# A decoder trunk on one core: two first sums over the memory interleaved by halves of their channels, and the fetches of constants and activations begun later

## The chip, the cores and the metric

The kernel runs on one core of one Trainium2 chip. The metric is the device time of one execution in microseconds (us). TensorE (PE in the profile) does the matrix products, VectorE (DVE), ScalarE (ACT) and GpSimd (POOL) the elementwise work, SyncE (SP) issues most of the transfers.

## The reference

Two layers over 1024 positions of 1024 channels. Each layer is a mixer (dilated attention with pooling in layer 0, a spatial gating unit with a state-space model in layer 1) and a cross-attention of four heads into 256 memory tokens. What the change touches is the memory side of that cross-attention and the first norm of x:

```
mem_n = rms_norm(mem, mem_norm)
kv = (mem_n @ w_kv).reshape(b, m, 2, X_HEADS, X_HEAD_DIM)
k, v = kv[:, :, 0], kv[:, :, 1]
sc = einsum('bshd,bmhd->bhsm', h @ w_q, k) * (X_HEAD_DIM ** -0.5)
p = softmax(sc); o = einsum('bhsm,bmhd->bshd', p, v); return o @ w_o
hn = rms_norm(x, norm_ab[0])     # layer 0's mixer starts from it
```

## The kernel before, in words

**Arithmetic.** Every matrix operand is split into a high and a low part, and a product is three matmuls: high by high, high by low, low by high (`mm3`, L206, L207, L208). For a weight, `split` makes the high part `wh` on ScalarE (L171, L180) and the low part `wl` on VectorE (L172, L181). For the memory, `norm_in` makes the pair `mg` (L226 on ScalarE, L227 on VectorE) for each of the eight channel blocks k.

**The prologue** does not need x. For both layers, `fold` multiplies the memory by `w_kv` (part 0: eight sums for the keys), folds `w_q` into the result, multiplies by the other half of `w_kv` (part 1: eight sums for the values), and folds `w_o` in. A sum over the memory is 24 matmuls of 256 columns: eight channel blocks of three. Results of the folding (`mo`, `vo`) are stored to HBM by ScalarE's queue. The sums rotate over three tags of PSUM with two banks each (`pm`, tags mm, s, o), so six sums can stand before the first bank has to be free again. A bank is freed when `kt` (L421, VectorE) has read it, and `kt` multiplies by `Rm`, the reciprocal norm of the memory. ScalarE and GpSimd then split `kt` into `ktr` (L213 and L214), the operand of the folding with `w_q`.

**Rm** comes from a chain: eight squares of the memory (`norm_sq`: L236 and L239 on ScalarE), seven additions on GpSimd (L243), and `norm_end` (L245 to L262): a high and low part (`acch`, `accl`), two matmuls with ones, logarithm and exponential on ScalarE, one multiplication on GpSimd, two steps on VectorE, the last at L262. The squares carry an ordering edge that puts them behind one chosen instruction of ScalarE, the high part of the first weight's second half.

**Weights** come in the order of a plan. `pump` loads up to `deep[0]` weights ahead of the last split and splits up to `deep[1]` ahead of the one in use; both are 5 in the prologue. Only the first weight is loaded in two halves of its channels (L158, 256 KB each) so that its first half can start early. The memory is fetched in four transfers of two channel blocks on ScalarE's queue (L366).

**Order.** The program is traced into a scheduler, which fixes the order on each engine from a simulated timeline and from the order of tracing; each engine then runs its list in order. `drive` interleaves the prologue with a side program, `pro_side`: one step of the side for every four yields of the main (rate 0.25). The prologue has 128 yields, thus 32 steps. `pro_side` lets one step pass, fetches the constants `cst` (L460), and then `load_x` fetches sixteen blocks of x (L474), one a step, splits them into `xg` (L226, L227), adds their squares, and makes the two norms with `norm_sum_pe` and `norm_sum_end` (two halves h of the positions). The reciprocal root of these norms is a chain of twelve operations on GpSimd (`rsqrt_aside`, L300 to L303), after which VectorE picks columns (L327, L329) and refines them (L289 to L293) into `Rt`. Layer 0's mixer (`ab_main`) uses `xg` in its first matmuls and `Rt` in copying their results out (L523): tiles 0 to 3 use the first half, tiles 4 to 7 the second.

Tiles of the pool tagged u (14 buffers) hold x, the squares, `kt`, `mo` and `vo` alike; a fetch of x waits until a buffer is free.

Of the kernel before, what the change touches and what calls it, by code (L numbers as in the profile page):

```python
# [8 lines left out]
F32 = mybir.dt.float32  # L9
F32R = mybir.dt.float32r  # L10
AF = mybir.ActivationFunctionType
ALU = mybir.AluOpType
# [5 lines left out]
NB = 42  # L18
# [80 lines left out]
class Prog:  # L99
# [49 lines left out]
            else:  # L149
                break  # L150

    def load(s, half=None):
        _, ap, w = s.plan[s.n_load]
        if half is not None:

            if half == 0:
                s.st[0] = s.pool.tile([128, 1024], F32, name="wst", tag="b", bufs=NB)
            s.nc.sync.dma_start(s.st[0][:, 512 * half:512 * half + 512], ap[:, 512 * half:512 * half + 512])  # L158
            s.n_load += half
            return  # L160
        t = s.pool.tile([128, 1024], F32, name="wst", tag="b", bufs=NB)
        s.last_load = s.nc.sync.dma_start(t[:, :w], ap() if callable(ap) else ap)
        s.st[s.n_load] = t
        s.n_load += 1

    def split(s, i, half=None):
        if half is not None:
            if half == 0:
                s.W[0] = [s.pool.tile([128, 1024], F32R, name=x, tag="b", bufs=NB) for x in ("wh", "wl")]
            c = slice(512 * half, 512 * half + 512)  # L170
            s.last_hi = s.nc.scalar.activation(s.W[0][0][:, c], s.st[0][:, c], AF.Copy)  # L171
            s.nc.vector.tensor_tensor(s.W[0][1][:, c], s.st[0][:, c], s.W[0][0][:, c], op=ALU.subtract)  # L172
            if half:
                s.st.pop(0)
                s.n_split += 1
            return
        t, w = s.st.pop(i), s.plan[i][2]
        H = s.pool.tile([128, 1024], F32R, name="wh", tag="b", bufs=NB)
        L = s.pool.tile([128, 1024], F32R, name="wl", tag="b", bufs=NB)
        s.last_hi = s.nc.scalar.activation(H[:, :w], t[:, :w], AF.Copy)  # L180
        s.nc.vector.tensor_tensor(L[:, :w], t[:, :w], H[:, :w], op=ALU.subtract)  # L181
        s.W[i] = (H, L)
        s.n_split += 1
# [175 lines left out]
    def constants(s):  # L359
        nc = s.nc  # L360
        s.gains = s.keep("gains", 72)
        nc.sync.dma_start(s.gains, s.a["gains"])
        s.memx = [s.b("mem0"), s.b("mem1")]
        for j in range(4):
            c = slice(512 * (j % 2), 512 * (j % 2) + 512)
            nc.scalar.dma_start(s.memx[j // 2][:, c], s.a["memT"][:, 512 * j:512 * j + 512])  # L366
            if j < 2:
                s.load(j)
        s.load()
        s.onef = s.keep("onef", 128)  # L370
        nc.vector.memset(s.onef, 1.0)
        s.ones = s.keep("ones", 128, F32R)
        nc.scalar.activation(s.ones, s.onef, AF.Copy)
        for h in range(2):
            s.R[h] = s.keep(f"R{h}", 512)
        s.Rt = s.keep("Rt", 8)
        s.mag8 = s.keep("mag8", 16)
        s.cst = s.keep("cst", C_END)
        s.ident = s.cst[:, C_ID:C_ID + 128]

    def memory(s):
        nc = s.nc
        st = {"g": G_MEM}
        mg = []
        xs = [s.memx[k // 4][:, 256 * (k % 4):256 * (k % 4) + 256] for k in range(8)]
        for k in range(8):
            if k in (2, 4):
                s.split(0, k // 2 - 1)
                first = s.last_hi
            if k % 2 == 0:  # L390
                t = s.b(f"mg{k}", F32R).rearrange("p (a b m) -> p a b m", a=2, b=2)
            mg.append((t[:, k % 2, 0], t[:, k % 2, 1]))
            s.norm_in(st, k, xs[k], 256, mg[-1], sq=False)
        s.pump()
        with s.tc.issue_after(first.ins):
            for k in range(8):
                s.norm_sq(st, k, xs[k], 256)
        s.memx = None
        s.mg = mg
        Rm = s.u("Rm")  # L400
        s.Rm = Rm[:, :256]
        s.mst = st

    def fold(s, l):

        nc = s.nc
        msc = s.dt(f"msc{l}", [2, 4, 128, 1024])
        vsc = s.dt(f"vsc{l}", [8, 128, 1024])
        s.msc[l], s.vsc[l] = msc, vsc
        for part in range(2):  # L410
            kt = []
            for d in range(8):
                key = ("kv", l, 8 * part + d)
                H, L = s.get(key)
                p = s.pm()
                yield from s.mm3(p[:, :256], [((H[:, 128 * k:128 * k + 128], L[:, 128 * k:128 * k + 128]), s.mg[k]) for k in range(8)])
                s.free(key)
                if l == 0 and part == 0 and d == 0:
                    s.norm_end(s.mst, s.Rm, 256)
                t = s.u("kt")  # L420
                nc.vector.scalar_tensor_tensor(t[:, :256], p[:, :256], 1.0 / 16 if part == 0 else 1.0, s.Rm, op0=ALU.mult, op1=ALU.mult)  # L421
                if d % 2 == 0:
                    o = s.b("ktr", F32R).rearrange("p (a b m) -> p a b m", a=2, b=2)
                kt.append((o[:, d % 2, 0], o[:, d % 2, 1]))
                s.hilo(kt[-1][0], kt[-1][1], t[:, :256], nc.gpsimd)
                yield 1
            if part == 0:
                for ct in range(8):
                    key = ("q", l, ct)
                    H, L = s.get(key)  # L430
                    for hp in range(2):
                        p = s.pm()
                        for h2 in range(2):
                            ds_ = [4 * hp + 2 * h2, 4 * hp + 2 * h2 + 1]
                            yield from s.mm3(p[:, 256 * h2:256 * h2 + 256], [((H[:, 128 * d:128 * d + 128], L[:, 128 * d:128 * d + 128]), kt[d]) for d in ds_])
                        t = s.u("mo")
                        nc.scalar.activation(t, p, AF.Copy)
                        nc.scalar.dma_start(msc[hp, ct // 2][:, 512 * (ct % 2):512 * (ct % 2) + 512], t)
                        yield 1
                    s.free(key)  # L440
            else:
                for h in range(4):
                    for oh in range(2):
                        key = ("o", l, 2 * h + oh)
                        H, L = s.get(key)
                        for mt in range(2):
                            p = s.pm()
                            yield from s.mm3(p, [((kt[2 * h + e][0][:, 128 * mt:128 * mt + 128], kt[2 * h + e][1][:, 128 * mt:128 * mt + 128]),
                                                  (H[:, 512 * e:512 * e + 512], L[:, 512 * e:512 * e + 512])) for e in range(2)])
                            t = s.u("vo")  # L450
                            nc.scalar.activation(t, p, AF.Copy)
                            kk = 2 * h + mt
                            nc.scalar.dma_start(vsc[4 * oh:4 * oh + 4, :, 128 * kk:128 * kk + 128].rearrange("c p o -> p c o"), t.rearrange("p (c o) -> p c o", c=4))
                            yield 1
                        s.free(key)

    def pro_side(s):
        yield 1
        with s.tc.issue_after(s.last_load.ins):
            s.nc.sync.dma_start(s.cst, s.a["cst"])  # L460
        yield from s.load_x()
# [5 lines left out]
    def load_x(s):  # L467

        s.xg = {}
        for h in range(2):  # L470
            st = {"g": G_AB}
            for k in range(8):
                x = s.u("x")
                s.nc.sync.dma_start(x, s.a["xT"][k][:, 512 * h:512 * h + 512])  # L474
                s.xg[k, h] = s.norm_in(st, k, x)
                yield 1
            s.norm_sum_pe(st)
            yield 1
            yield 1
            s.norm_sum_end(st, s.Rt[:, 4 * h:4 * h + 4], s.R[h], True)  # L480
            yield 1
# [1137 lines left out]
```

## Time and profile before

| what | us |
| --- | --- |
| three timed runs | 2034.98, 2037.51, 2039.67 |
| their median | 2037.51 |
| the profiled execution, its own time | 2035.52 |
| its span, first to last instruction | 2033.8 |

The span is what the trace shows; 1.7 us of the profiled execution's time lie outside it. Starts in the rows below count from the span's start. In a timeline a row gives start, duration, engine, source line, operation, tile written and tiles read, shape and count; in brackets stands how long the engine had been idle and what released it. Rows of several instructions are merged, their duration is that of the group. A matmul's duration runs into the next one's, so the pace is read from the starts.

### The profile page before, as it was taken

Reading aid. Unit: us, or ns where it says so; the run is one execution under the profiler, and the core shown is the slowest. Engines: PE = TensorE matmul, PEld = TensorE weight load, DVE = VectorE, ACT = ScalarE, POOL = GpSimd, SP = SyncE. Lnnn points to the kernel's source line nnn. Section 1 sums busy time; section 2 is a strip of 40 time slices with the busy share of each in tenths; the row PEclk is TensorE's granted clock in tenths of the full one; section 3 lists DMA queues with packets and bytes.
Section 4 is the critical chain, followed back from the end, with each engine's and each line's share of the span. In section 5 each row is a group of like instructions: output and inputs, shape, how many; then the busy total and the mean of one; then the engine's idle time right before and its main releaser. Section 6 shows DMA issues by size and latency. Waiting matters only on the chain.

```text
span 2033.8 us, 31759 instructions
## 1 busy us (share of the span) xinstructions
PE 2007.1 (99%) x12294; PEld 1672.7 (82%) x12294; DVE 1139.0 (56%) x2011; ACT 803.6 (40%) x1625; POOL 571.3 (28%) x829
## 2 busy tenths in 40 slices
PE   8999999999999999999999999999999999999998
PEld 7999877777787768888888888788888888888888
DVE  7686055655666685555445557644653334655544
ACT  7776134455345452123333444122221133434454
POOL 4564007932344373231111013211211101220013
PEclk9999999999999999999999999999999999999999
DMA  7988302213122222236533145423322225641142
GB/s 290 309 311 284 99 25 70 71 56 122 53 85 83 71 74 96 86 123 232 183 130 125 42 169 187 152 83 103 125 83 78 75 91 189 199 159 62 65 161 83
DMA packets 129160, 258.67 MB, mean 127 GB/s; under 512 B 12785, under 2 KB 58993, under 8 KB 129009
## 3 DMA queue, kind: packets, MB, share of 16 engines
q1 hardware_dynamic: 86032, 188.47, 27.6%
q0 software_dynamic: 13440, 43.53, 5.8%
q10 hardware_dynamic: 29536, 24.65, 3.8%
q8 instruction: 96, 1.57, 0.3%
q14 instruction: 56, 0.45, 0.1%
HBM read 193.16 MB, written 63.44 MB: 126 GB/s over the span
## 4 chain that ended last, share of the span: by engine, by line
PE 94%; DVE 2%; ACT 1%; DMA 1%; POOL 1%; issue 0%; ACTq 0%; SPq 0%; DVEq 0%; POOLq 0%
PE ps_mm L206 14%; PE ps_mm L208 14%; PE ps_mm L207 14%; PE ps_s L207 5%; PE ps_s L208 5%; PE ps_s L206 5%; PE ps_o L206 4%; PE ps_o L207 4%; PE ps_o L208 4%; PE ps_s L577 2%; PE ps_mm L1390 1%; PE ps_mm L1392 1%; PE ps_mm L1391 1%; PE ps_o L634 1%; PE ps_o L893 1%; PE ps_o L891 1%
## 5 line engine op out<-in xcount | busy, mean ns | idle before, releaser
L181 DVE TENSOR_TENSOR wl<-wst,wh 128x1024 fp32r<-128x1024 f32 (+1 forms) x263 | 348.8, 1340 | 87.4 <-ACT wh L180 79.6
L206 PE MATMUL ps_mm<-xg,wh 128*128 128x512 f32 x928 | 368.8, 397 | 1.2 <-DVE xd L1366 1.2
L208 PE MATMUL ps_mm<-xg,wl 128*128 128x512 f32 x928 | 361.8, 390 | 0.0
L207 PE MATMUL ps_mm<-xg,wh 128*128 128x512 f32 x928 | 361.8, 390 | 0.0
L180 ACT ACTIVATE wh<-wst 128x1024 fp32r<-128x1024 f32 (+1 forms) x263 | 262.8, 1016 | 112.2 <-PE ps_mm L207 96.9
L206 PEld LDWEIGHTS ps_mm<-xg,wh 128*128 128x128 f32 x928 | 174.2, 188 | 44.4 <-issue 7.7
L208 PEld LDWEIGHTS ps_mm<-xg,wl 128*128 128x128 f32 x928 | 174.2, 188 | 37.1 <-issue 0.2
L207 PEld LDWEIGHTS ps_mm<-xg,wh 128*128 128x128 f32 x928 | 174.4, 188 | 34.0 <-issue 0.2
L243 POOL TENSOR_TENSOR acc<-acc,sq 128x512 f32<-128x512 f32 (+1 forms) x81 | 104.6, 1292 | 196.0 <-ACT sq L239 190.9
L226 ACT ACTIVATE xg<-x,gains 128x512 fp32r<-128x512 f32 x64 | 46.1, 721 | 235.4 <-DVE x L831 182.1
L589 ACT ACTIVATE P<-P,mx 128x192 f32<-128x192 f32 (+7 forms) x128 | 66.1, 517 | 142.9 <-DVE mx L588 138.3
L621 ACT ACTIVATE PTr<-ps_t 128x128 f32<-128x128 f32 (+2 forms) x192 | 40.2, 268 | 119.9 <-DVE PT L617 117.5
L227 DVE SCALAR_TENSOR_TENSOR xg<-x,gains,xg 128x512 fp32r<-128x512 f32 x64 | 57.6, 900 | 42.0 <-ACT xg L226 42.0
L584 DVE TENSOR_TENSOR P<-ps_s,cst 128x320 f32<-128x320 f32 (+7 forms) x128 | 65.6, 549 | 15.5 <-PE ps_s L577 6.7
L1418 DVE TENSOR_TENSOR ug<-ps_mm,R 128x512 f32<-128x512 f32 x32 | 22.1, 689 | 89.1 <-PE ps_mm L208 89.0
L617 DVE TENSOR_TENSOR PT<-ps_t,cst 128x256 f32<-128x256 f32 (+1 forms) x128 | 46.1, 399 | 41.6 <-PE ps_t L611 32.4
L206 PE MATMUL ps_s<-gr,wh 128*128 128x512 f32 x168 | 65.5, 390 | 0.0
L208 PE MATMUL ps_s<-gr,wl 128*128 128x512 f32 x168 | 65.5, 390 | 0.0
L207 PE MATMUL ps_s<-gr,wh 128*128 128x512 f32 x168 | 65.4, 389 | 0.0
L591 ACT ACTIVATE P<-P,den 128x192 f32<-128x192 f32 (+7 forms) x128 | 61.3, 511 | 7.6 <-DVE den L590 7.4
L239 ACT ACTIVATE sq<-x 128x512 f32<-128x512 f32 (+1 forms) x77 | 44.7, 582 | 43.0 <-DVE x L939 36.4
L213 ACT ACTIVATE pt<-ps_t 128x128 fp32r<-128x128 f32 x128 | 34.7, 276 | 66.4 <-DVE pt L214 45.5
(455 smaller groups left out, 4912.4 us busy)
## 6 DMA issues: line engine op xcount, KB each, us to landing
wst<-w_ab SPq DMA_DIRECT2D x40, 512.0 KB, 3.8
wst<-w_out_ab SPq DMA_DIRECT2D x32, 512.0 KB, 3.8
wst<-vsc SPq DMA_DIRECT2D x32, 512.0 KB, 3.8
wst<-w_kv SPq DMA_DIRECT2D x31, 512.0 KB, 6.4
wst<-w_cd SPq DMA_DIRECT2D x24, 512.0 KB, 3.4
wst<-w_out_cd SPq DMA_DIRECT2D x32, 384.0 KB, 3.4
wst<-w_q SPq DMA_DIRECT2D x16, 512.0 KB, 6.8
msc<-mo ACTq DMA_DIRECT2D x32, 256.0 KB, 6.7
```

The lines of the kernel that those rows point to most:

```text
L180: s.last_hi = s.nc.scalar.activation(H[:, :w], t[:, :w], AF.Copy)
L181: s.nc.vector.tensor_tensor(L[:, :w], t[:, :w], H[:, :w], op=ALU.subtract)
L206: s.nc.tensor.matmul(ps, lhsT=lh, rhs=rh, start=(i == 0), stop=False)
L207: s.nc.tensor.matmul(ps, lhsT=lh, rhs=rl, start=False, stop=False)
L208: s.nc.tensor.matmul(ps, lhsT=ll, rhs=rh, start=False, stop=(i == n - 1))
L226: nc.scalar.activation(H, x, AF.Copy, scale=g)
L227: nc.vector.scalar_tensor_tensor(L, x, g, H, op0=ALU.mult, op1=ALU.subtract)
L243: nc.gpsimd.tensor_tensor(st["acc"][:, :n], st["acc"][:, :n], q[:, :n], op=ALU.add)
L584: nc.vector.tensor_tensor(t[:, :n], p[e][:, :n], s.cst[:, m0:m0 + n], op=ALU.add)
L589: j = nc.scalar.activation(t[:, :m], t[:, :m], AF.Exp, bias=mx, accum_out=den)
L591: k = nc.scalar.activation(t[:, :m], t[:, :m], AF.Copy, scale=den)
L617: nc.vector.tensor_tensor(PT[b // 2, e][:, c0 + 128 * j0:c0 + 256].rearrange("p (j i) -> p j i", i=128), src, s.cst[:, C_NM + 128 * j0:C_N ...
```

## The change

It does four things. The loading and splitting in halves goes to any weight i, and the first two weights are loaded in the order first half of 0, first half of 1, second half of 0, second half of 1. In `memory`, ScalarE's list gets the two first halves between the memory's blocks and the two second halves behind them, and the squares get their ordering edge to the last high part that has been traced when they are, which stands behind `pump`: `pump` has traced the splits of the third and fourth weight by then. In `fold`, the first two sums of layer 0 are traced as one block: channel blocks 0 to 3 of both, then 4 to 7 of both, in two banks. In `pro_side`, eight steps pass before the constants are fetched, and each fetch of x gets an ordering edge to the last weight load traced.

```diff
-    def load(s, half=None):
-        _, ap, w = s.plan[s.n_load]
-        if half is not None:
+    def load(s, i=None, half=0):
+        if i is not None:
 
             if half == 0:
-                s.st[0] = s.pool.tile([128, 1024], F32, name="wst", tag="b", bufs=NB)
-            s.nc.sync.dma_start(s.st[0][:, 512 * half:512 * half + 512], ap[:, 512 * half:512 * half + 512])
+                s.st[i] = s.pool.tile([128, 1024], F32, name="wst", tag="b", bufs=NB)
+            s.nc.sync.dma_start(s.st[i][:, 512 * half:512 * half + 512], s.plan[i][1][:, 512 * half:512 * half + 512])
             s.n_load += half
             return
+        _, ap, w = s.plan[s.n_load]
...
@@ split: the same with s.W[i], s.st[i] for s.W[0], s.st[0]
...
@@ constants
             nc.scalar.dma_start(s.memx[j // 2][:, c], s.a["memT"][:, 512 * j:512 * j + 512])
-            if j < 2:
-                s.load(j)
+            s.load(j % 2, j // 2)
         s.load()
...
@@ memory
             if k in (2, 4):
-                s.split(0, k // 2 - 1)
-                first = s.last_hi
+                s.split(k // 2 - 1, 0)
...
+        for i in range(2):
+            s.split(i, 1)
         s.pump()
-        with s.tc.issue_after(first.ins):
+        with s.tc.issue_after(s.last_hi.ins):
             for k in range(8):
                 s.norm_sq(st, k, xs[k], 256)
...
@@ fold
-                H, L = s.get(key)
-                p = s.pm()
-                yield from s.mm3(p[:, :256], ...)
+                if l == part == 0 and d < 2:
+
+                    if d == 0:
+                        two = [(s.get(("kv", 0, i)), s.pm()) for i in range(2)]
+                        for k0 in (0, 4):
+                            for (H, L), p in two:
+                                for k in range(k0, k0 + 4):
+                                    c = slice(128 * k, 128 * k + 128)
+                                    nc.tensor.matmul(p[:, :256], lhsT=H[:, c], rhs=s.mg[k][0], start=(k == 0), stop=False)
+                                    nc.tensor.matmul(p[:, :256], lhsT=H[:, c], rhs=s.mg[k][1], start=False, stop=False)
+                                    nc.tensor.matmul(p[:, :256], lhsT=L[:, c], rhs=s.mg[k][0], start=False, stop=(k == 7))
+                    p = two[d][1]
+                    yield 1
+                else:
+                    H, L = s.get(key)
+                    p = s.pm()
+                    yield from s.mm3(p[:, :256], ...)
...
@@ pro_side, load_x
-        yield 1
+        for _ in range(8):
+            yield 1
         with s.tc.issue_after(s.last_load.ins):
             s.nc.sync.dma_start(s.cst, s.a["cst"])
...
-                s.nc.sync.dma_start(x, s.a["xT"][k][:, 512 * h:512 * h + 512])
+                with s.tc.issue_after(s.last_load.ins):
+                    s.nc.sync.dma_start(x, s.a["xT"][k][:, 512 * h:512 * h + 512])
```

## Rows read from the trace of the kernel before

**Rows 1.** The page: busy time of each engine, share of the span, instructions.

```profile
PE 2007.1 (99%) x12294; PEld 1672.7 (82%) x12294; DVE 1139.0 (56%) x2011; ACT 803.6 (40%) x1625; POOL 571.3 (28%) x829
```

**Rows 2.** Waits of TensorE, whole span: total us, times, longest.

```profile
PE ps_s L206 <- ACT wh L171: 6.4, 1, 6.4
PE ps_s L206 <- ACT mg L226: 2.5, 1, 2.5
...
PE ps_mm L208 <- DVE wl L181: 1.7, 1, 1.7
```

**Rows 3.** Timeline, TensorE: first matmul, after the gap, around 17.5, seventh sum.

```profile
6.39 0.58 PE L206 MATMUL ps_s<-mg,wh 128*128 128x256 f32 x1 [6.39 <-ACT wh L171]
...
10.79 0.58 PE L206 MATMUL ps_s<-mg,wh 128*128 128x256 f32 x1 [2.46 <-ACT mg L226]
...
17.31 0.41 PE L207 MATMUL ps_mm<-mg,wh 128*128 128x256 f32 x1
17.52 0.36 PE L208 MATMUL ps_o<-mg,wl 128*128 128x256 f32 x1
...
31.98 0.28 PE L208 MATMUL ps_s<-mg,wl 128*128 128x256 f32 x1
```

**Rows 4.** Windows: length, busy us (count) of PE, PEld, DVE, ACT, POOL; PEclk, DMA, GB/s.

```profile
10.80:17.50 6.70, 6.41 (x22) 5.28 (x23) 6.70 (x8) 6.70 (x14) 4.43 (x6) 1.00 1.03 415
17.50:32.00 14.50, 14.50 (x123) 14.50 (x122) 10.85 (x16) 10.18 (x16) 5.81 (x5) 1.00 1.03 408
```

**Rows 5.** DMA, issued at 1.74, 2.2, 2.2 and about 4.7: size, us to landing.

```profile
wst<-w_kv SPq DMA_DIRECT2D x1, 256.0 KB, 6.7
...
wst<-w_kv SPq DMA_DIRECT2D x1, 512.0 KB, 8.2
mem<-memT ACTq DMA_DIRECT2D x1, 256.0 KB, 8.4
...
wst<-w_kv SPq DMA_DIRECT2D x1, 512.0 KB, 8.3
```

**Rows 6.** Instructions by tile or line, until 60 us: ns min/median/max, first and last start.

```profile
L227 DVE SCALAR_TENSOR_TENSOR mg<-mem,gains,mg x8: 481/947/992, 4.9 to 15.1; 128x256 fp32r<-128x256 f32 x8
...
L243 POOL TENSOR_TENSOR acc<-acc,sq x11: 722/793/2278, 9.8 to 52.3; 128x256 f32<-128x256 f32 x7, 128x512 f32<-128x512 f32 x4
...
L214 POOL TENSOR_TENSOR ktr<-kt,ktr x8: 746/1420/1725, 26.3 to 38.9; 128x256 fp32r<-128x256 f32 x8
```

**Rows 7.** Timeline of the norm's chain on ScalarE, GpSimd and VectorE.

```profile
9.03 0.40 ACT L236 ACTIVATE acc<-mem 128x256 f32<-128x256 f32 x1
...
12.39 3.34 POOL L243 TENSOR_TENSOR acc<-acc,sq 128x256 f32<-128x256 f32 x4 [0.19 <-ACT sq L239]
...
13.88 1.99 ACT L180 ACTIVATE wh<-wst 128x1024 fp32r<-128x1024 f32 x2
...
18.21 0.41 DVE L214 TENSOR_TENSOR accl<-acc,acch 128x256 fp32r<-128x256 f32 x1
...
24.88 0.42 DVE L262 SCALAR_TENSOR_TENSOR Rm<-nt,Rm 128x256 f32<-128x256 f32 x1
```

**Rows 8.** Timeline around TensorE's third wait.

```profile
108.21 1.76 DVE L327 TENSOR_TENSOR nt<-nv,cst 128x512 f32<-128x512 f32 x1 [3.27 <-POOL R L303]
...
113.68 0.38 PE L208 MATMUL ps_mm<-mg,wl 128*128 128x256 f32 x1 [1.71 <-DVE wl L181]
```

**Rows 9.** The fetches of x by tile; SyncE's waits until 220 us.

```profile
L474 SPq DMA_DIRECT2D x<-xT x16: 327/328/1157, 13.1 to 122.8; - x16
...
SPq L474 <- DMA vsc<-vo: 14.0, 3, 10.6
```

**Rows 10.** Timeline: the last step of the second Rt; the mixer's first two copies out.

```profile
177.89 0.16 DVE L293 SCALAR_TENSOR_TENSOR Rt<-rc 128x4 f32<-128x4 f32 x1
...
204.78 0.69 ACT L523 ACTIVATE vt<-ps_s,Rt 128x512 f32<-128x512 f32 x1 [1.58 <-PE ps_s L515]
...
210.22 0.69 ACT L523 ACTIVATE vt<-ps_o,Rt 128x512 f32<-128x512 f32 x1 [4.75 <-PE ps_o L515]
```

More of the change, by code (lines that the diff above doesn't have):

```diff
@@ L168, in split @@
             if half == 0:
-                s.W[0] = [s.pool.tile([128, 1024], F32R, name=x, tag="b", bufs=NB) for x in ("wh", "wl")]
+                s.W[i] = [s.pool.tile([128, 1024], F32R, name=x, tag="b", bufs=NB) for x in ("wh", "wl")]
             c = slice(512 * half, 512 * half + 512)
-            s.last_hi = s.nc.scalar.activation(s.W[0][0][:, c], s.st[0][:, c], AF.Copy)
-            s.nc.vector.tensor_tensor(s.W[0][1][:, c], s.st[0][:, c], s.W[0][0][:, c], op=ALU.subtract)
+            s.last_hi = s.nc.scalar.activation(s.W[i][0][:, c], s.st[i][:, c], AF.Copy)
+            s.nc.vector.tensor_tensor(s.W[i][1][:, c], s.st[i][:, c], s.W[i][0][:, c], op=ALU.subtract)
             if half:
-                s.st.pop(0)
+                s.st.pop(i)
                 s.n_split += 1
@@ L413, in fold @@
                 key = ("kv", l, 8 * part + d)
-                H, L = s.get(key)
-                p = s.pm()
-                yield from s.mm3(p[:, :256], [((H[:, 128 * k:128 * k + 128], L[:, 128 * k:128 * k + 128]), s.mg[k]) for k in range(8)])
+                if l == part == 0 and d < 2:
[13 more added lines that the diff above has]
+                    p = s.pm()
+                    yield from s.mm3(p[:, :256], [((H[:, 128 * k:128 * k + 128], L[:, 128 * k:128 * k + 128]), s.mg[k]) for k in range(8)])
                 s.free(key)
```

## The prediction

> **What bounds the kernel now.** I read the page's busy times first, then TensorE's waits, then the timeline of the first 40 us engine by engine. TensorE is busy in 99% of the span [rows 1], so a change elsewhere pays only where TensorE stands or runs slowly. The list of its waits shows where that is: 6.4 us before the first matmul, 2.5 us soon after, and a third wait of 1.7 us near 112 us [rows 2]; the others lie in later stages, which the change doesn't touch. The timeline and the windows add what a list of waits can't show. Before 17.5 us the matmuls of 256 columns start 0.21 us apart, which is TensorE's level of 1.2 GHz; afterwards 123 of them take 14.5 us, 0.118 us each, the level of 2.4 GHz [rows 3, 4]. The column of the granted clock reads 1.00 in both windows, so here the level must be read from the starts. From 10.8 to 17.5 us only 22 matmuls ran, 0.30 us each, in the rhythm of VectorE's low parts of the memory [rows 4, 6]. The head of the kernel is thus the place to gain: 6.4 us of waiting for the first weight, a hole of 2.5 us, and some 7 us at low pace.
>
> **The interleaved sums.** The first matmul stays at 6.39: it needs the first half of weight 0 and the first memory block, and both are still issued first. What changes is what stands behind the first six matmuls. Before, the next operand came from a ScalarE list in which squares stood ahead of the memory's high parts; now no square stands there, and the second SyncE transfer is the first half of weight 1, which should land where the second half of weight 0 landed, at 1.74 + 6.7 = 8.4 us [rows 5]. So 24 matmuls over channel blocks 0 to 3 are ready by about 10 us, and the hole, 8.33 to 10.79 [rows 3], closes.
>
> Size: before, 6 + 22 = 28 matmuls are done at 17.52, when the pace doubles [rows 3, 4]. From 8.33 without a hole the 28th ends at 8.33 + 22 x 0.213 = 13.0. If the pace doubles there too, the head gains 17.5 - 13.0 = 4.5 us. Lower bound: the pace doubles only after the 48 matmuls of both sums. They then end at 8.33 + 42 x 0.213 = 17.3, against 17.52 + 20 x 0.118 = 19.9 before, a gain of 2.6. Upper bound: the operands. The last memory transfer lands at 2.2 + 8.4 = 10.6 and weight 1, with both second halves now in its place, at 2.2 + 8.2 = 10.4 [rows 5]. Behind it ScalarE has two memory blocks and two halves, 1,536 columns, at least 1.5 us by the 1.0 us for 1,024 columns [rows 7]; 0.6 for the low part, then 11 matmuls, 1.3: 14.0, a gain of 5.9. I take 4.5 because the load before the rise would be denser than before, not thinner.
>
> **The squares, moved.** This edit costs something. The ordering edge now leads to the high part of weight 3, not to that of weight 0. Weight 3 lands at 4.7 + 8.3 = 13.0 [rows 5], its high part takes 1.0, and ScalarE's own list (10.6 + 1.5 + 2.0 for two whole weights) gives 14.1 as well. I take 14.5 for the first square, 9.03 before [rows 7]. Two squares, 0.7, and seven additions at 0.79 each [rows 6] end at 20.7; before, the last ended at 15.73. From there to the end of `Rm` it took 9.6 us (15.73 to 25.30) [rows 7], so `Rm` stands at 30.3. Early bound: 14.0, additions at 0.72, and no lateness of `accl`, which ran 2.5 us after the last addition though the high part needs 0.4: 27.3. Late bound: two further high parts of weights between the squares, 2.0: 32.3.
>
> Who waits? All sums before are held in banks until `kt` multiplies by `Rm`. Six sums fit; the seventh was in full swing at 31.98 with its first bank long free [rows 3]. With the head's gain it wants the bank at 31.98 - 4.5 = 27.5, and gets it one `kt` (0.4) after `Rm`, at 30.7. TensorE waits 3.2 us, and of the 4.5 us only 32.0 - 30.7 = 1.3 are left. Bounds: 4.3 with the early `Rm`, and a loss of 0.7 with the late one.
>
> Next in line is `ktr`. Six `kt` come at once, and GpSimd takes 0.75 to 1.42 us for each low part [rows 6]. From 31.6 the sixth is ready at 36.1 or at 40.1. TensorE ends the eighth sum at 30.7 + 2 x 2.84 = 36.4 and needs the fifth and sixth 12 matmuls later, at 37.8. Cost 0 to 2.3; I take 1.0, nearer to the short end because the additions for x, which shared GpSimd and VectorE there, have gone.
>
> **The fetches, moved.** In the trace 16 fetches of x run from 13.1 to 122.8 [rows 9], 18 side steps, 6.1 us each; seven steps more are 43 us. Early on this takes 16 fetches' competition out of the head, but SyncE's weights come fast enough there anyway (no wait of TensorE between 17.5 and 111 [rows 2, 4]): nothing. The third wait, 1.7 us at 111.98, has a visible cause: VectorE stood 3.27 us for GpSimd's root chain, then did L327 for 1.76, with the low part of a weight queued behind, for which TensorE waited [rows 8]. That tail moves to about 151 us, into the folding of layer 1's `w_q`. Gone from the old place: 1.7 (or 0, if another weight is late there). At the new place the same tail stands before other low parts: 0 to 1.7, taken as 0.8, since VectorE's lead in weights decides and no row shows it there.
>
> The end of the second `Rt`, 178.05, moves to 220.8. It is first needed by tile 4's copy at 204.78 + 4 x 5.44 = 226.5 [rows 10]: covered by 5 us, and a late copy would first use up the other banks. Constants go with x and are needed by the same tail. Traced steps: 30 of 32 are used, so the side still ends inside the prologue. The two extra half transfers on SyncE replace a whole one, with the same bytes: nothing.
>
> **Sum.** -4.5 + 3.2 + 1.0 - 1.7 + 0.8 = -1.2 us. The profiled execution took 2035.5 us (span 2033.8 plus 1.7 outside), 2.0 below the median of the runs; so 2034.3 for a run like it, 2036.3 for the median.
>
> **Rivals.**
>
> *The chain of squares is hidden.* If `Rm` comes near 27.3 and `ktr` at the short rate, the head keeps 4.3 and the third wait goes: -4.3 - 1.7 + 0.5 = -5.5, 2032.0. For it speak the 2 us of slack in `accl`; against it, that weight 3's landing at 13.0 can't come earlier.
>
> *The chain becomes the bound of the head* (the other side). The squares wait for two more weights (2.0) and `accl` stands behind two more low parts (2.0): `Rm` at 34.3, bank at 34.7, TensorE waits 7.2 us. That is 2.7 later than before, plus 2.3 for `ktr`; it takes 28 matmuls at the low pace afterwards, 28 x 0.095 = 2.7, to make +7.7, 2045; without that and without the third wait +3.3, 2041. It decides for slower from `Rm` at about 33 on.
>
> *The wait costs the clock.* Even the 3.2 us of the forecast may put TensorE back to 1.2 GHz. After the hole of 2.46 us the pace stayed low for 22 matmuls [rows 3, 4]; no row shows a fall from the high pace. 28 matmuls at the low pace would cost 2.7 us, giving 2039.0. The Trainium skill, "TensorE: Matmul & The Clock Gate", Part 1, says that idleness takes the array's clock back to half and activity restores it; by that rule the sum would be +1.5 instead of -1.2. The trace shows only the rise.
>
> *The later fetches hold up weights.* SyncE once stood 10.6 us before a fetch of x until a store had freed a buffer [rows 9], with weights queued behind. In the new places fetches again meet the stores of both foldings. Up to 9 weights of 2.8 us are traced ahead, 25 us; two such stops and a landing (21.2 + 8.3 = 29.5) overrun them by 4.5: +3.3 to +5, 2041.5. One stop alone is covered, as before.
>
> **How the numbers follow.** The forecast has 0.46, the hidden chain 0.22, the chain as bound 0.13, the clock 0.10, the fetches 0.09. About 0.2%, 4.1 us, is what can be told from no change here (2033.4 to 2041.6). Faster: nearly all of the hidden chain and a little of the forecast's early end, 0.22. Slower: most of the bound chain and half of the fetches, 0.16. Same: 0.62. The range reaches from the hidden chain, 2031.5, to the lower half of the slower cases, 2042.0. The likeliest case alone spans 2033 to 2039: `Rm` between 28.5 and 32.3, `ktr` between 0 and 2.3, third wait gone or not.
>
> **What would show it.** In the changed profile: TensorE without a hole between 8.3 and 15 us, the pace doubling near 13; the first square near 14.5 and `Rm` near 30; a wait of about 3 us of TensorE on `kt`, or on the matmuls with ones, which stand in its list, around 27; no wait at 112; L327 near 151; the last fetch of x near 165 and the first `vt` unhindered. It is wrong if the squares run before weight 3's high part, if the pace rises late, or if a wait of over 3 us appears after 60 us.

## The result and the profile after

The changed kernel takes 2048.12 us (median of six runs, 2047.29 to 2049.66), the kernel before, measured beside it, 2037.02: ratio 1.0056, 95% interval 1.0045 to 1.0066. It is 11 us slower, outside the stated range. The profiled execution took 2047.69 us, its span is 2046.0, 12.2 more than before.

All of the 12.2 us is there before layer 0's mixer starts. First matmul of each stage, read from TensorE's timeline:

| stage | before | after | difference |
| --- | --- | --- | --- |
| folding with `w_q`, layer 0 | 37.51 | 39.13 | +1.6 |
| value sums, layer 0 | 60.55 | 62.17 | +1.6 |
| key sums, layer 1 | 105.83 | 107.26 | +1.4 |
| folding with `w_q`, layer 1 | 130.82 | 134.93 | +4.1 |
| value sums, layer 1 | 154.31 | 166.37 | +12.1 |
| mixer of layer 0 | 199.14 | 211.68 | +12.5 |

Two stages lose it: layer 1's key sums 2.7 us, layer 1's folding with `w_q` 8.0 us. The head, which was to gain, loses 1.6. TensorE's waits until 215 us (total, times, longest), against [rows 2]:

```profile
PE ps_s L422 <- ACT wh L171: 6.8, 1, 6.8
PE ps_mm L208 <- DVE wl L181: 4.2, 2, 3.7
PE ps_s L206 <- ACT wh L180: 2.8, 1, 2.8
PE ps_mm L206 <- ACT vo L465: 1.8, 1, 1.8
PE ps_s L206 <- ACT ktr L213: 1.5, 2, 0.9
PE ps_o L208 <- DVE wl L181: 1.1, 1, 1.1
...
```

The hole of 2.5 us has gone; in its place stand a wait of 2.8 us and later ones that before knew only as one of 1.7.

**The head** did at first what was forecast. TensorE's timeline, against [rows 3]:

```profile
12.18 0.39 PE L424 MATMUL ps_o<-mg,wl 128*128 128x256 f32 x1
12.39 0.30 PE L422 MATMUL ps_s<-mg,wh 128*128 128x256 f32 x1
...
26.93 0.28 PE L208 MATMUL ps_mm<-mg,wl 128*128 128x256 f32 x1
...
29.96 0.58 PE L206 MATMUL ps_s<-mg,wh 128*128 128x256 f32 x1 [2.76 <-ACT wh L180]
```

Matmuls run without a hole from 6.80, the pace doubles at 12.4 instead of 17.5, and six sums are done at 27.05, where TensorE then stands. The chain behind the squares, on ScalarE, GpSimd and VectorE, against [rows 7]:

```profile
13.26 0.41 ACT L236 ACTIVATE acc<-mem 128x256 f32<-128x256 f32 x1
...
28.87 1.04 ACT L180 ACTIVATE wh<-wst 128x1024 fp32r<-128x1024 f32 x1
```

```profile
14.06 7.96 POOL L243 TENSOR_TENSOR acc<-acc,sq 128x256 f32<-128x256 f32 x7 [13.54 <-ACT sq L239]
```

```profile
27.62 0.43 DVE L262 SCALAR_TENSOR_TENSOR Rm<-nt,Rm 128x256 f32<-128x256 f32 x1
28.09 0.42 DVE L435 SCALAR_TENSOR_TENSOR kt<-ps_s,Rm 128x256 f32<-128x256 f32 x1
```

The first square starts at 13.26 and `Rm` ends at 28.05. The bank is free at 28.5, but TensorE waits until 29.96, for the high part of weight 6, which stands in ScalarE's list behind the first `ktr`, which needs `kt` and so `Rm`. And the pace falls. Windows (length, busy times, PEclk, DMA, GB/s), against [rows 4]:

```profile
30.00:36.00 6.00, 5.41 (x24) 5.11 (x25) 5.80 (x5) 5.23 (x9) 5.71 (x4) 0.50 0.54 199
...
159.30:166.40 7.10, 7.05 (x47) 7.06 (x48) 6.79 (x16) 1.54 (x3) 0.15 (x1) 0.77 0.95 320
```

From 30 to 36 us the granted clock is 0.50, which is 1.2 GHz: 24 matmuls in 6 us. The two sums from 29.96 to 39.13 take 9.2 us, where 48 matmuls of 0.12 take 5.8; 0.6 of the 3.4 us is a second wait, at 31.35.

**Around 112 us** ScalarE stands for a block of x, and what is behind it in its list is late:

```profile
105.64 1.07 ACT L180 ACTIVATE wh<-wst 128x1024 fp32r<-128x1024 f32 x1
105.96 0.68 ACTq L467 DMA_DIRECT2D vsc<-vo  x1
112.22 0.72 ACT L226 ACTIVATE xg<-x,gains 128x512 fp32r<-128x512 f32 x1 [5.50 <-DMA x<-xT]
112.84 0.61 ACT L239 ACTIVATE sq<-x 128x512 f32<-128x512 f32 x1
113.36 1.04 ACT L180 ACTIVATE wh<-wst 128x1024 fp32r<-128x1024 f32 x1
114.31 0.57 ACT L465 ACTIVATE vo<-ps_mm 128x512 f32<-128x512 f32 x1
```

```profile
114.94 0.39 PE L206 MATMUL ps_mm<-mg,wh 128*128 128x256 f32 x1 [1.77 <-ACT vo L465]
116.00 0.39 PE L208 MATMUL ps_mm<-mg,wl 128*128 128x256 f32 x1 [0.56 <-DVE wl L181]
123.10 0.39 PE L208 MATMUL ps_o<-mg,wl 128*128 128x256 f32 x1 [1.07 <-DVE wl L181]
```

SyncE issued that block at 106.12. ScalarE was ready for it at 106.7 and stood for 5.5 us; the weight's high part and the copy of a bank (`vo`) stood behind it, and TensorE waited first for the copy, then for two low parts.

**Around 155 us** two engines stand. VectorE waits for GpSimd's root chain, at the place that was forecast (151); a weight's low part is behind it, and TensorE waits 3.7 us:

```profile
155.34 1.75 DVE L327 TENSOR_TENSOR nt<-nv,cst 128x512 f32<-128x512 f32 x1 [6.46 <-POOL R L303]
157.01 2.28 DVE L181 TENSOR_TENSOR wl<-wst,wh 128x1024 fp32r<-128x1024 f32 x1
```

```profile
159.34 0.58 PE L208 MATMUL ps_mm<-ktr,wl 128*128 128x256 f32 x1 [3.68 <-DVE wl L181]
```

Then the clock is at 0.77 in the mean for 7 us. Three waits for `ktr`, 2.1 us between 137 and 142, come on top in the same stage. ScalarE waits again for x, 6.04 us before 164.86. Over the prologue ScalarE's waits for x grow from 3.1 us (3 waits) to 19.1 (6):

```profile
ACT xg L226 <- DMA x<-xT: 19.1, 6, 6.0
```

The transfers themselves are hardly slower: median 5.0 us from issue to landing, 4.5 before. What is later is the issue, by the place in SyncE's list: with the edge the second fetch stands behind 31 transfers of weights and the last behind 65, without it (run 5 below) behind 29 and 63. The fetches of x, first and last issue, here and in run 5:

```profile
L490 SPq DMA_DIRECT2D x<-xT x16: 327/377/1194, 60.6 to 181.2; - x16
L489 SPq DMA_DIRECT2D x<-xT x16: 327/328/848, 60.4 to 164.8; - x16
```

This leaves three suspects: the new head, whose late `Rm` holds the seventh sum (theory A); the eight steps (theory B; rival D is its form for GpSimd's root chain); the ordering edge on x (theory C).

### The profile page after: what moved, and what is told of

The parts are those of the page before. It is cut to its first block, busy times and chain, and to the rows that moved or that the text cites. A ratio compares the mean times of both kernels' runs of the same rounds, so it can differ in the third digit from the quotient of the medians.

```text
span 2046.0 us, 31765 instructions
## 1 busy us (share of the span) xinstructions
PE 2010.7 (98%) x12294; PEld 1675.8 (82%) x12294; DVE 1143.8 (56%) x2012; ACT 803.8 (39%) x1626; POOL 576.6 (28%) x829
## 4 chain that ended last, share of the span: by engine, by line
PE 88%; DVE 3%; POOL 2%; ACT 1%; issue 1%; DMA 0%; ACTq 0%; DVEq 0%; POOLq 0%
PE ps_mm L206 14%; PE ps_mm L208 13%; PE ps_mm L207 13%; PE ps_s L206 4%; PE ps_s L208 4%; PE ps_s L207 4%; PE ps_o L207 3%; PE ps_o L206 3%; PE ps_o L208 3%; PE ps_s L593 2%; PE ps_mm L1406 1%; PE ps_mm L1408 1%; PE ps_mm L1407 1%; PE ps_o L650 1%; PE ps_o L909 1%; PE ps_o L908 1%
## 5 line engine op out<-in xcount | busy, mean ns | idle before, releaser
L181 DVE TENSOR_TENSOR wl<-wst,wh 128x1024 fp32r<-128x1024 f32 (+1 forms) x262 | 358.6, 1386 | 91.2 <-ACT wh L180 86.8
L227 DVE SCALAR_TENSOR_TENSOR xg<-x,gains,xg 128x512 fp32r<-128x512 f32 x64 | 52.2, 815 | 43.2 <-ACT xg L226 43.2
L678 POOL DMA_DIRECT2D gab<-G x32 | 18.4, 576 | 150.9 <-DMA s5par<-s_p 48.2
```

The lines of the kernel that those rows point to most:

```text
L227: nc.vector.scalar_tensor_tensor(L, x, g, H, op0=ALU.mult, op1=ALU.subtract)
```

## The experiments

Each ratio is against the kernel before on the same chip, with its 95% interval.

**1. Squares one step earlier.** Changed kernel, with the edge taken before `pump`:

```diff
             s.split(i, 1)
+        first = s.last_hi
         s.pump()
-        with s.tc.issue_after(s.last_hi.ins):
+        with s.tc.issue_after(first.ins):
```

> The changed kernel, but with the memory's squares ordered behind the second half of weight 1 (the high part traced last before the loads and splits that follow), not behind the high part of weight 3. Theory A, the late Rm holds the seventh sum and the wait puts the pace back to 1.2 GHz: first square near 11.5, Rm near 25, no wait of TensorE near 27 us, matmuls 0.12 us apart from 12 to 39 us, the folding with w_q starts near 33 instead of 39.1, and the time falls from 2048.1 by 5 to 6.5 us to about 2042. Rival, the wait at 27 us belongs to the high part of weight 6, which stands late in ScalarE's list whatever Rm does: the wait of 2.8 us stays and the time stays within 1.5 us of 2048.

Measured 2044.65, ratio 1.0039 (1.0025 to 1.0053). The edit hardly moved the chain: first square at 12.44, `Rm` at 28.5, since the seven additions, three of them now beside low parts of weights, took 8.2 us. The wait for weight 6 is 1.3 us and the folding begins in earnest at 39.1, as in the changed kernel. It doesn't test theory A; most of what it gains lies near 159 us, where the wait is 1.8 us instead of 3.7.

**2. Fetches early again, edge kept.** Changed kernel with `yield 1` for the eight:

> The changed kernel, but the side program lets one step pass before the constants, as before the change; the ordering edge of the x fetches behind the last weight load stays, and so does the head. Theory B, the seven steps are what costs time after 40 us (the root chain on GpSimd and the x blocks then fall into the foldings of layer 1): the waits of TensorE at 115 to 123 and 137 to 159 us go, 10 of the 12.2 us come back, about 2038. Rival, the edge costs it (x lands late because it is issued behind weights, and ScalarE, whose list has x in it, holds up the weights' high parts): the time stays above 2044 and waits on ScalarE or VectorE remain between 50 and 170 us.

Measured 2051.28, ratio 1.0074 (1.0059 to 1.0089). Theory B falls: with the steps as before the change the kernel is slower still. The waits move with the fetches (2.2 us at 72, 7.5 us at 121).

**3. Fetches late, old head.** Kernel before, with eight steps and the edge:

> The kernel before with only the fetches moved: eight steps and the ordering edge, the head untouched. If the parts add up, theory B expects the start at about 37.5 us for the folding with w_q, as before, and the layer 1 waits of the changed kernel: 2037.0 + 10.6 = 2047.6. If the fetches only hurt together with the new head (other list, other landing times), it is within 3 us of 2037.

Measured 2048.29, ratio 1.0057 (1.0042 to 1.0072). The number is that of theory B, but the run contains the edge too; what it shows is that the whole loss is in the fetches, not in the head.

**4. New head with both.** Run 1 and run 2 together:

> The interleaved sums alone, with the squares ordered early as in the first run of this set and one side step as before the change (the edge of the x fetches stays). If theories A and B hold and add up: 2037.0 less the head's gain of about 4.5 = 2032.5, faster than the kernel before by 0.2%. If the interleaving itself is worth nothing later on (the gain is given back at the next wait, ktr on GpSimd), 2036 to 2038.

Measured 2049.42, ratio 1.0062 (1.0047 to 1.0077). Missed by 17 us: the edge was still in it, and run 7 shows the same kernel without it.

**5. No edge.** Changed kernel, eight steps:

```diff
-                with s.tc.issue_after(s.last_load.ins):
-                    s.nc.sync.dma_start(x, ...)
+                s.nc.sync.dma_start(x, ...)
```

> The changed kernel without the ordering edge on the fetches of x; eight steps still pass first, the head is as changed. Theory C, the edge costs the time after 100 us (x is issued behind the weights, lands after ScalarE's list has come to it, and the weights' high parts behind it are late): ScalarE's waits for x fall from over 18 us to under 5, the waits of TensorE at 115 to 123 us go, and 5 to 10 us come back, 2038 to 2043. Rival D, the eight steps cost it by putting GpSimd's root chain where VectorE has no lead: the wait of 3.7 us at 159 us stays and the time stays above 2044.

Measured 2037.47, ratio 1.0006 (0.9997 to 1.0016). Without the ordering edge 10.6 us come back (2048.12 - 2037.47; 10.2 by the two ratios, each against the kernel before on its own chip), to the time of the kernel before and just under the range of theory C. Rival D falls with it: the eight steps are still in.

**6. The edge alone.** Kernel before, with the edge of the diff and nothing else:

> The kernel before with nothing but the ordering edge on the fetches of x; one step passes, the head is untouched. Theory C: slower than before by 8 to 14 us, 2045 to 2051, with ScalarE waiting more than 12 us for x. Rival D: within 2 us of 2037, since the steps are as before.

Measured 2049.43, ratio 1.0065 (1.0048 to 1.0082). The edge alone costs the whole. ScalarE's waits for x (until 215 us), in this run:

```profile
ACT xg L226 <- DMA x<-xT: 22.0, 8, 6.2
```

and in the run without the edge:

```profile
ACT xg L226 <- DMA x<-xT: 4.5, 2, 2.6
```

**7. New head alone.** Run 4 without the edge:

> The interleaved sums alone: the squares ordered behind the second half of weight 1, one step, no edge on x; only the head differs from the kernel before. Theory C with a head that gives back what it wins: the folding with w_q starts within 2 us of 37.5 and the time is 2034 to 2039. If the head's early work keeps its lead, 2032 to 2034. If the time is over 2044, neither edge nor steps are the cause and the new order of the head upsets the later lists by itself.

Measured 2037.48, ratio 1.0004 (0.9994 to 1.0013). The head gives back what it wins. Nine kernels now stand in two rows: with the edge 2044.7 to 2051.3, without it 2037.0 to 2037.5, whatever head and steps are.

**8. Root chain on VectorE.** Changed kernel, first half:

```diff
-            s.norm_sum_end(st, s.Rt[...], s.R[h], True)
+            s.norm_sum_end(st, s.Rt[...], s.R[h], h == 1)
```

> The changed kernel with the first half's root chain as VectorE instructions (the three steps of rsqrt) instead of GpSimd's twelve; the second half keeps GpSimd's. Where VectorE stood 6.5 us for GpSimd and TensorE then 3.7 us, it now works some 6 to 9 us itself. If the wait for GpSimd is the cause of that stall, the 3.7 us wait near 159 us and the low pace after it shrink and 3 to 6 us come back, 2042 to 2045; if x's late landing is the cause, ScalarE's wait of 6 us there remains and the time stays within 2 us of 2048.

Measured 2048.09, ratio 1.0056 (1.0041 to 1.0071). The stall at 159 us goes, the time does not: ScalarE still waits 20.6 us for x, and TensorE loses the time at 115 to 125 us (4.8 us of waits, 3.4 in the changed kernel, then 3.2 us at a granted clock of 0.50) and in 1.8 us of waits at 170 to 171. GpSimd's chain decided only where the loss fell.

**9. Use x a step later.** Changed kernel with its edge and its steps; only the use moves:

```diff
-            for k in range(8):
-                x = s.u("x")
+            xs = []
+            for k in range(9):
+                if k < 8:
+                    xs.append(s.u("x"))
...
-                s.xg[k, h] = s.norm_in(st, k, x)
-                yield 1
+                if k:
+                    s.xg[k - 1, h] = s.norm_in(st, k - 1, xs[k - 1])
+                if k < 8:
+                    yield 1
```

> The changed kernel with its ordering edge and its eight steps, but each block of x is used one side step (four yields, some 6 us) after the step that fetches it; the ninth use goes with the norm's sum. Theory C, in its narrower form (x lands after ScalarE's list has come to it, and what stands behind in that list is late): ScalarE's waits for x fall from 19 us to under 6, and most of the 10.6 us comes back, 2038 to 2042. Rival E, the edge costs through SyncE's list (a fetch that waits for a free buffer holds the weights behind it): the time stays above 2045, since the fetches keep their places there.

Measured 2036.48, ratio 1.0003 (0.9993 to 1.0012). ScalarE's waits for x are gone from the list altogether, with the fetches still behind the weights: SyncE's list is that of the changed kernel but for one place, where a fetch and a weight have swapped. Rival E falls, and the narrower form of theory C holds.

**10. An older edge.** Changed kernel, each fetch behind the load that was last a step before:

```diff
+        behind = s.last_load
...
-                with s.tc.issue_after(s.last_load.ins):
+                with s.tc.issue_after(behind.ins):
...
+                behind = s.last_load
```

> The changed kernel, but each fetch of x is ordered behind the weight load that was the last one traced a side step (some 6 us, two weights) earlier. If what counts is how late x is issued, the loss shrinks by degrees: 2040 to 2045, with ScalarE's waits for x between 6 and 15 us. If the edge as such upsets the lists, whatever it points to, the time stays within 2 us of 2048.

Measured 2036.31, ratio 1.0002 (0.9992 to 1.0011). The loss is all gone, with 4.0 us of ScalarE's waits for x left, none over 1.6. But the run doesn't grade the edge: SyncE, VectorE, GpSimd and TensorE run the lists of run 5, instruction for instruction, and ScalarE does but for the places of a few stores. The older edge asks for an order that stood already, so this is run 5 once more, and whether the loss grows by degrees stays open.

**11. Two more splits before the norm's end.** Run 5 (no edge), and

```diff
                 if l == 0 and part == 0 and d == 0:
+                    s.deep = (5, 7)
+                    s.pump()
+                    s.deep = (5, 5)
                     s.norm_end(s.mst, s.Rm, 256)
```

> The changed kernel without the edge on x (2037.5), and with two weights more split ahead just before the norm's end is traced, so that the high part of weight 6 stands in ScalarE's list before the parts that wait for Rm. If the wait of 2.8 us before the seventh sum and the 0.9 us after it belong to that high part, they shrink to the wait for the bank (Rm at 28.1 to 28.5, one kt later, TensorE there at 27: 1.5 us), the low pace of the 28 to 35 us stretch may go with it, and 2 to 5 us come back: 2032.5 to 2035.5. If Rm alone decides, the start of the folding with w_q stays near 39 us and the time within 1.5 us of 2037.5.

Measured 2037.21, ratio 1.0002 (0.9993 to 1.0011). The wait for weight 6 became one for `kt`, 2.9 us, since `Rm` came at 31.2, 2.4 us later than in run 5: 1.4 of it because more low parts ran beside GpSimd's additions, the rest because TensorE came to the second matmul with ones only at 26.59. The folding starts at 37.56, 1.6 us before run 5, and gives 1.4 of that back at a wait for `ktr`. Moving the high part alone is worth nothing in the time. After the wait for `kt` the pace did not fall, though it was no shorter than the 2.76 us of the changed kernel:

```profile
31.71 0.39 PE L206 MATMUL ps_s<-mg,wh 128*128 128x256 f32 x1 [2.92 <-DVE kt L438]
...
31.70:37.50 5.80, 5.79 (x48) 5.79 (x49) 5.36 (x9) 4.87 (x10) 5.32 (x5) 1.00 0.47 177
```

**12. The same, with early squares.** Run 11, and the squares' edge taken after the first halves:

```diff
                 s.split(k // 2 - 1, 0)
+                first = s.last_hi
...
-        with s.tc.issue_after(s.last_hi.ins):
+        with s.tc.issue_after(first.ins):
```

> As the run before, and the squares ordered behind the first half of weight 1 instead of behind the third weight traced after it, which lets them run between the memory's blocks. If both the high part of weight 6 and Rm have to be early: Rm near 25 to 26, no wait at 27 us, folding with w_q from 33 to 35 us, 2031 to 2034. If early squares push the memory's low parts back as in the kernel before (GpSimd's additions beside them), the head loses 1 to 3 us again in the first 17 us and the time is no better than the run before.

Measured 2033.10, ratio 0.9984 (0.9974 to 0.9993): faster than both, and in the expected range. The squares run from 9.16, the additions end at 16.05, `Rm` at 28.0 (25 to 26 expected), and TensorE's waits until 215 us are

```profile
PE ps_s L423 <- ACT wh L171: 6.3, 1, 6.3
PE ps_s L424 <- DVE mg L227: 1.2, 3, 0.7
PE ps_s L208 <- DVE wl L181: 0.6, 1, 0.6
```

The start pays 1.2 us of waits for the squares, and after them the clock:

```profile
12.00:15.60 3.60, 2.23 (x12) 1.43 (x10) 3.60 (x5) 3.60 (x8) 3.29 (x5) 1.00 1.03 414
15.70:19.00 3.30, 3.30 (x16) 3.29 (x17) 3.30 (x4) 3.30 (x5) 0.36 (x1) 0.50 1.04 413
```

Six sums so end only at 30.95, 1.0 us before the kernel before and 3.9 after the changed kernel, and find a bank free: no wait at 27 us is left, though `Rm` comes no earlier than in the changed kernel (28.05). The run is faster, but it doesn't show that an earlier `Rm` is why. In its trace the folding with `w_q` starts at 36.71, 0.8 us before the kernel before, and the mixer at 197.37, 1.8 before; in between, the old wait of 1.7 us at 112 is missing.

## Why the prediction was wrong, point by point

**The step that failed** is "The fetches, moved": the ordering edge was costed at nothing, in fact not named. The text counted the seven steps' delay, said that SyncE's weights come fast enough, and looked for harm only in SyncE's list, in a rival that priced a fetch holding up weights. The harm is on the other side. The edge puts a fetch up to two weights later in SyncE's list, so that it is issued close to when ScalarE's list comes to its use. ScalarE then stands up to 6 us for it, with high parts of weights and copies of banks behind; their lead is used up, and TensorE waits. Price: 12.5 us alone (run 6 against its kernel before, 2049.43 - 2036.9), 10.6 in the changed kernel (2048.12 - 2037.47), nothing once the use is a step later (run 9). The transfer itself took 5.0 us at the median, 4.5 before: not its length but the place of its use set the price. Without the edge the last fetch is issued at 164.8, as forecast (165), with it at 181.2, a part of which is the loss itself.

**The third wait.** Its place was right (L327 at 155, forecast 151), its price was not: 3.7 us and a lower clock after it, forecast 0.8; a wait of over 3 us after 60 us was the forecast's own sign of being wrong. Without the edge the same chain made VectorE wait 12.6 us in all (run 5), and TensorE's only wait after 40 us is 1.5, inside the 0 to 1.7 of the forecast. It costs more, it seems, only where ScalarE's waits have used up the lead; that this is the link is inferred from runs 5 and 8.

**The head's gain** was right: the pace doubles at 12.4 (forecast 13.0), six sums end 4.9 us sooner (forecast 4.5). The moment of the rise is no fixed thing: in runs 2, 5, 8, 9 and 10, whose head is the same, it lies between 9.5 and 13.3, but six sums end within 1 us of the changed kernel in all of them. **The wait for `Rm`** was right in size, 2.8 + 0.6 us against 3.2. `Rm` came at 28.05, not 30.3: the squares started 1.2 us sooner than forecast and from the last addition to `Rm` it took 6.0 us instead of 9.6, in part because `accl` did not stand behind low parts. Both outweighed the additions, 7.96 us for seven where 0.79 each was taken. The releaser was another, the high part of weight 6, which hangs on `Rm` by its place in the list.

**The clock** was a rival at 0.10 and came true, at 2.8 us (9.2 against 5.8 for two sums, less the second wait of 0.6; forecast 2.7). The Trainium skill, "TensorE: Matmul & The Clock Gate", Part 1, says that idleness takes the array to half its clock; the changed kernel agrees with its 0.50 after a wait of 2.76 us, and run 11 shows a wait of 2.92 us without a fall. The head so came out at +1.6 where -0.3 was forecast (-4.5 + 3.2 + 1.0). `ktr` did not cost its 1.0 here; it cost 2.1 us in layer 1, which the forecast didn't have.

**The additions' price** was a mean of two kinds. In the changed kernel three of the seven overlap a low part of a weight, `wl`, and take 1.35, 1.60 and 1.60 us; the other four take 0.73 to 0.74. The `wl` pay too, up to 1.75 us instead of 1.2. One of each:

```profile
16.80 1.32 DVE L181 TENSOR_TENSOR wl<-wst,wh 128x1024 fp32r<-128x1024 f32 x1 [1.99 <-ACT wh L180]
17.12 1.60 POOL L243 TENSOR_TENSOR acc<-acc,sq 128x256 f32<-128x256 f32 x1
...
20.48 0.73 POOL L243 TENSOR_TENSOR acc<-acc,sq 128x256 f32<-128x256 f32 x1
```

The Trainium skill, "SBUF — State Buffer", section "Who interferes with whom", says that a VectorE instruction with two SBUF inputs contends with a GpSimd one that reads SBUF. The trace agrees: `wl` reads two tiles, and only the additions beside it are long. The forecast's 0.79 came from additions beside the memory's low parts [rows 6], which read two tiles as well but are shorter; there VectorE paid, 0.95 us for most low parts instead of the 0.48 that they take in the changed kernel with no addition beside them.

Neither the direction nor the forecast's own range held. What the sum said of head and third wait would have given a time within 0.2% of before, and that is what the change measures without the edge. That agreement is partly luck: the head came out 1.9 us worse than forecast in run 5 too, where the folding with `w_q` starts at 39.15.

## What to carry to other kernels

An ordering edge on a transfer is priced at the instruction that uses it: read where that stands in its engine's list, and what is queued behind it there. Where a transfer is put later, put its use later by the same amount; one step was enough here. A faster head is worth only what the next dependent chain lets through: six sums ended 4.9 us sooner, and all of it went into the wait for the chain that frees the banks and the low clock after it. The order that did gain 3 us gave up most of the early start; what its gain rests on is not shown.

## What the runs showed of the hardware

A wait of TensorE of some 2.8 us may or may not cost the clock: granted 0.50 afterwards in the changed kernel and, after 2.75 to 2.76 us at the same place, in runs 2, 5, 8, 9 and 10; granted 1.00 after 2.92 us in run 11. Shorter waits can come before a fall too: 0.50 in run 12 after waits of 0.7, 0.25 and 0.26 us. And the granted clock read 1.00 at the start of every kernel (6 to 9 us) while the starts of the matmuls showed 1.2 GHz; only later falls appear in that column.

An addition of GpSimd took 0.73 us with no `wl` of VectorE beside it and up to 1.60 beside one, in the same stretch of one kernel.
